# Delta-rule layer: the even halves of the merged blocks and the decayed keys are scaled on ScalarE instead of GpSimd

## The chip, the cores and the metric

The program runs on one core of one Trainium2 chip. The metric is the device time of one execution in microseconds. In the tables of the profile PE is TensorE (PEld its weight loads), DVE is VectorE, ACT is ScalarE, POOL is GpSimd and SP is SyncE, which issues the DMAs of this part.

## What is computed

A block of four mixers (convolution, softmax attention with forget gates, gated delta rule, sliding window) and then a second block, all on 512 positions and width 1024. The change lies in the gated delta rule alone, which is third. Cut to what matters:

```python
GDN_HEADS, GDN_HEAD_DIM, GDN_CHUNK = 8, 128, 64

def gdn_mixer(h, w_in, w_conv, a_log, dt_bias, w_onorm, w_out):
    proj = h @ w_in                                   # q, k, v, z, beta, a
    qkv = jax.nn.silu(causal_conv(qkv, w_conv))
    q = q * lax.rsqrt(jnp.sum(q * q, -1, keepdims=True) + EPS) * (1.0 / math.sqrt(d))
    k = k * lax.rsqrt(jnp.sum(k * k, -1, keepdims=True) + EPS)
    ...
    o = chunk_gated_delta(q, k, v, g, beta)
    o = o * lax.rsqrt(jnp.mean(o * o, -1, keepdims=True) + EPS) * w_onorm
    return (o.reshape(B_, S, GDN_WIDTH) * jax.nn.silu(z)) @ w_out

def chunk_gated_delta(q, k, v, g, beta):              # per head
    L = strict_lower((k * beta) @ k.T * decay)
    T = triangular_solve(eye + L, eye)                # inverse of a unit triangle
    u, w = T @ (v * beta), T @ (k * beta * exp(g_cum))
    k_dec = k * exp(g_last - g_cum)                   # the decayed keys
    def step(state, ...):
        v_new = u_c - w_c @ state
        o = (q * exp(g_cum)) @ state + qk_c @ v_new
        state = state * exp(gl) + k_dec.T @ v_new
```

## The kernel before

Activations lie feature-major, as eight tiles of 128 by 512. A projection from a weight column block is 24 matmuls of 128x512: for each of eight input tiles three products (lines 328 to 330), because both sides are split into a high and a low part (the weights by a cast on ACT, `whi`, and a subtraction on DVE, `wlo`). Such matmuls are called projection matmuls below.

`gdn_layer` goes through eight heads, with four blocks of 128 positions (NT = 4) where the chunks of 64 of the reference have become 128. For a head it projects, convolves and transposes the keys (`kt`), takes their norm (`ssk` on DVE, the power `rk` on POOL), scales them (`kn`, the tile `y`, line 765 on ACT), transposes them back (`knt`, then `knT`) and forms `kk`, the products of the keys with themselves. From these comes the strictly lower matrix `dc`. It is inverted in two parts.

`block_inverses` takes the 16x16 blocks on the diagonal: they are packed (`d1`, `d2`, line 870), sent to DRAM and read back spread over the partitions (the DMAs `dd` and `lb`), and solved column by column in 60 small DVE steps (lines 882 and 884), which leave `X`.

`unit_inverse_T` merges the blocks in three levels, s = 16, 32 and 64. At each level the new `X2` has an even half, which is the old X scaled by a column of ones and zeros (line 897), and an odd half, scaled likewise (line 918 on ACT; in the first level it is part of line 916 on DVE) and then corrected by products on TensorE (`Dt`, `z` and `e` in the first level, `dz` and `e` in the others). The tile of the last level is called `E`.

Then a recurrence over the four blocks: `ks` from the state S, `r` on DVE (line 812), `vn` from E and r, `ds` from the decayed `kn` (line 776 has scaled it by `kd`) and vn, the next S on DVE (line 824, the first one on ACT), and `o`. The outputs are scaled by `ro` (a power on POOL) into `on` (line 839), transposed (`ot`), and gated with `z`.

The instructions stand in program order on no engine: a scheduler lays out one in-order queue for each engine ahead of time from its own costs and the dependences. `issue_after` holds the inversion back until the projections of its head are issued, so that inversions and recurrences of one head lie between projections of the next. Each engine then works its queue strictly in turn, and an instruction that waits holds up all behind it.

Heads are numbered here from the first to the eighth. The program's own tile numbers (`X_6840`) are not the same in the two kernels.

Of the kernel before, what the change touches and what calls it, by code (L numbers as in the profile page):

```python
# [12 lines left out]
AF = mybir.ActivationFunctionType  # L13
# [5 lines left out]
P = 128  # L19
# [3 lines left out]
NT = 4  # L23
# [219 lines left out]
class KB:  # L243
# [419 lines left out]
    def gdn_layer(self):  # L663
        nc = self.nc
# [42 lines left out]
        v4 = lambda a: a.rearrange("p (t d) -> p t d", t=NT)  # L707
# [3 lines left out]
        blk = [slice(t * P, (t + 1) * P) for t in range(NT)]  # L711
# [26 lines left out]
        for hd in range(H):  # L738
# [6 lines left out]
            kd = self.small([P, NT], "kd")  # L745
# [17 lines left out]
            kn = kT  # L763
# [9 lines left out]
                c = blk[t]  # L773
                nc.vector.scalar_tensor_tensor(dc[:, c], kk[:, c], nb[:, t, hd:hd + 1], dc[:, c], ALU.mult, ALU.mult)
            X = self.block_inverses(dc)
            nc.gpsimd.tensor_mul(v4(kn)[:, :NT - 1], v4(kn)[:, :NT - 1], kd[:, :NT - 1].unsqueeze(2).to_broadcast([P, NT - 1, P]))

            vT, _ = conv_silu(2, hd)
            vps = self.t4(vT, "vt")
# [107 lines left out]
    def unit_inverse_T(self, N, X):  # L887

        nc = self.nc
        v4 = lambda a: a.rearrange("p (t d) -> p t d", t=NT)
        off = self.small([P, S], "off", 1)
        nc.gpsimd.tensor_mul(v4(off), v4(N), self.con("off16").unsqueeze(1).to_broadcast([P, NT, P]))
        for s in (16, 32, 64):
            X2 = self.big("E", shape=[P, NT, P]) if s == 64 else self.small([P, NT, 2 * s], f"X{2 * s}", 1)
            nc.gpsimd.tensor_scalar_mul(X2[:, :, :s], X, self.con(f"even{s}"))
            if s == 16:

                full = self.small([P, S], "full", 1)  # L900
                nb = P // s
                nc.vector.tensor_mul(full.rearrange("p (t b i) -> p t b i", t=NT, i=s), X.unsqueeze(2).to_broadcast([P, NT, nb, s]),
                                     self.con(f"bd{s}").rearrange("p (b i) -> p b i", i=s).unsqueeze(1).to_broadcast([P, NT, nb, s]))
                ps = self.t4(full, "Dt")
                Dm = self.small([P, S], "Dm", 1)
                nc.scalar.copy(Dm, ps)
                zp = self.att("z")
                z = self.small([P, NT * s], "zt", 1)
                for t in range(NT):
                    nc.tensor.matmul(zp[:, t * s:(t + 1) * s], off[:, t * P:(t + 1) * P], X[:, t], start=True, stop=True)  # L910
                nc.scalar.copy(z, zp[:, :NT * s])
                ep = self.att("e")
                for t in range(NT):
                    nc.tensor.matmul(ep[:, t * s:(t + 1) * s], Dm[:, t * P:(t + 1) * P], z[:, t * s:(t + 1) * s], start=True, stop=True)
                ev = ep[:, :NT * s].rearrange("p (t c) -> p t c", t=NT)
                nc.vector.scalar_tensor_tensor(X2[:, :, s:], X, self.con(f"odd{s}"), ev, ALU.mult, ALU.add)
            else:
                nc.scalar.activation(X2[:, :, s:], X, AF.Copy, scale=self.con(f"odd{s}"))
                dz = self.att("dz")
                Dz = self.small([P, S], "Dm", 1)  # L920
                rows = [(slice(r, r + s), slice(r, r + 2 * s)) for r in range(0, P, 2 * s)]
                w = NT * s
                for lo, pair in rows:
                    for t in range(NT):
                        c = slice(t * s, (t + 1) * s)
                        nc.tensor.matmul(dz[lo, c], X[pair, t], self.ident[pair, lo], start=True, stop=True)  # L926
                        c = slice(w + t * s, w + (t + 1) * s)
                        nc.tensor.matmul(dz[lo, c], N[pair, t * P + lo.start:t * P + lo.stop], X2[pair, t, s:], start=True, stop=True)  # L928
                    nc.scalar.copy(Dz[lo, :2 * w], dz[lo, :2 * w])
                ep = self.att("e")  # L930
                for lo, pair in rows:
                    for t in range(NT):
                        c = slice(t * s, (t + 1) * s)
                        nc.tensor.matmul(ep[lo, c], Dz[lo, c], Dz[lo, w + t * s:w + (t + 1) * s], start=True, stop=True)
                    nc.scalar.copy(X2[lo, :, s:], ep[lo, :w].rearrange("p (t c) -> p t c", t=NT))
            X = X2
        return X.rearrange("p t c -> p (t c)")
# [596 lines left out]
```

## Time and profile before

| | before |
|---|---|
| median of 3 runs | 2088.7 us (2084.69 to 2089.15) |
| the profiled execution | 2088.03 us, its span 2086.3 us |
| delta-rule heads, 505 to 905 us of the span | 400.0 us |
| PE, DVE, ACT, POOL busy in it | 371.4, 265.0, 236.4, 102.8 us |
| mean granted TensorE clock in it | 0.94 |

Busy time says how much an engine did. Which engine sets the time is read from TensorE's waits and from the granted clock: a matmul takes as many cycles in either case and twice as long at half clock.

### The profile page before, as it was taken

The numbers are of one execution on the slowest core, as the hardware profiler recorded it, in microseconds if no ns is written. First come the engines' busy times: TensorE is split into PE (matmuls) and PEld (weight loads), VectorE is DVE, ScalarE is ACT, GpSimd is POOL, SyncE is SP. The second block draws the span as 40 slices with busy tenths as digits, with TensorE's granted clock in tenths as the row PEclk, the third lists the DMA queues.
The fourth block names the chain that finished last, engine by engine and source line by source line (L and its number), as shares of the span: only waits on it lengthen the run. The fifth ranks groups of instructions, "written<-read, shape, count | busy, mean of one in ns | idle before, by whom it ended". The sixth has DMA issues, their size and how long they took to land.

```text
span 2086.3 us, 25930 instructions
## 1 busy us (share of the span) xinstructions
PE 2026.5 (97%) x9810; PEld 1592.0 (76%) x9810; DVE 1213.0 (58%) x2420; ACT 886.7 (43%) x1640; POOL 164.3 (8%) x178
## 2 busy tenths in 40 slices
PE   8999999999899988999999999999999999999999
PEld 6888787777777766778667767776788878888887
DVE  5545445555876765465765546644544467878621
ACT  4222343344776553453565454356622243322211
POOL 0000000000333221100001101000011100000000
PEclk9999999999999997999999999999999999999999
DMA  5233432225322221153114412120232342332331
GB/s 183 92 101 117 137 110 78 85 72 175 87 78 65 65 75 31 52 179 98 50 41 157 123 59 93 61 81 31 71 101 92 99 165 93 99 101 92 111 121 66
DMA packets 64508, 197.69 MB, mean 95 GB/s; under 512 B 8412, under 2 KB 8796, under 8 KB 64384
## 3 DMA queue, kind: packets, MB, share of 16 engines
q1 hardware_dynamic: 63440, 193.57, 28.9%
q0 software_dynamic: 800, 2.25, 0.4%
q8 instruction: 77, 1.26, 0.3%
q14 instruction: 47, 0.39, 0.1%
q10 hardware_dynamic: 144, 0.22, 0.0%
HBM read 183.13 MB, written 12.89 MB: 94 GB/s over the span
## 4 chain that ended last, share of the span: by engine, by line
PE 61%; DVE 5%; ACT 4%; DMA 2%; POOL 2%; issue 1%; POOLq 0%; SPq 0%; ACTq 0%; DVEq 0%
PE pj L330 16%; PE pj L328 16%; PE pj L329 16%; DMA lb<-dd 2%; PE s L1042 1%; PE z L1404 1%; DVE tmp L882 1%; PE o L1095 1%; PE pt L1086 1%; DVE X L884 1%; DVE wlo L223 1%; POOL rk L659 1%; PE dz L926 1%; PE tm L328 0%; PE dz L928 0%
## 5 line engine op out<-in xcount | busy, mean ns | idle before, releaser
L328 PE MATMUL pj<-hh,whi 128*128 128x512 f32 (+2 forms) x1528 | 609.1, 399 | 7.6 <-ACT hh L342 7.6
L329 PE MATMUL pj<-hl,whi 128*128 128x512 f32 (+2 forms) x1528 | 611.2, 400 | 1.2 <-DVE hl L343 1.2
L330 PE MATMUL pj<-hh,wlo 128*128 128x512 f32 (+2 forms) x1528 | 609.3, 399 | 2.0 <-DVE wlo L223 2.0
L222 ACT CAST whi<-raw 128x1024 fp32r<-128x1024 f32 x301 | 313.7, 1043 | 663.9 <-PE pj L329 417.3
L223 DVE TENSOR_TENSOR wlo<-raw,whi 128x1024 fp32r<-128x1024 f32 x301 | 375.5, 1248 | 203.5 <-ACT whi L222 197.2
L328 PEld LDWEIGHTS pj<-hh,whi 128*128 128x128 f32 (+2 forms) x1528 | 288.1, 189 | 68.3 <-ACT hh L342 8.0
L330 PEld LDWEIGHTS pj<-hh,wlo 128*128 128x128 f32 (+2 forms) x1528 | 288.3, 189 | 64.8 <-issue 4.3
L329 PEld LDWEIGHTS pj<-hl,whi 128*128 128x128 f32 (+2 forms) x1528 | 288.4, 189 | 62.7 <-issue 3.6
L328 PE MATMUL pj<-gh,whi 128*128 128x512 f32 x432 | 170.7, 396 | 0.5 <-ACT gh L339 0.3
L329 PE MATMUL pj<-gl,whi 128*128 128x512 f32 x432 | 170.7, 396 | 0.0
L330 PE MATMUL pj<-gh,wlo 128*128 128x512 f32 x432 | 170.6, 396 | 0.0
L634 DVE SCALAR_TENSOR_TENSOR y<-u,cols,y 128x512 f32<-128x512 f32 x160 | 123.0, 769 | 2.4
L328 PEld LDWEIGHTS pj<-gh,whi 128*128 128x128 f32 x432 | 81.0, 188 | 20.4 <-ACT whi L222 1.1
L329 PEld LDWEIGHTS pj<-gl,whi 128*128 128x128 f32 x432 | 81.0, 188 | 18.7 <-DVE gl L340 0.4
L330 PEld LDWEIGHTS pj<-gh,wlo 128*128 128x128 f32 x432 | 81.1, 188 | 18.4 <-DVE wlo L223 0.4
L473 DVE TENSOR_TENSOR x<-pj,x 128x512 f32<-128x512 f32 x48 | 33.1, 691 | 93.9 <-PE pj L330 93.9
L328 PE MATMUL pj<-whi,hh 128*128 128x512 f32 x168 | 66.4, 398 | 0.0
L329 PE MATMUL pj<-wlo,hh 128*128 128x512 f32 x168 | 66.1, 394 | 0.0
L330 PE MATMUL pj<-whi,hl 128*128 128x512 f32 x168 | 65.7, 392 | 0.0
L1435 DVE TENSOR_TENSOR gt<-pj,rb 128x512 f32<-128x512 f32 x24 | 16.5, 690 | 64.1 <-PE pj L330 64.1
L882 DVE TENSOR_TENSOR tmp<-lb,X 128x30 f32<-128x30 f32 (+14 forms) x240 | 43.7, 214 | 11.8 <-DMA lb<-dd 11.8
L1466 DVE TENSOR_TENSOR u<-pj,rb 128x512 f32<-128x512 f32 x44 | 30.5, 693 | 30.5 <-PE pj L330 28.7
(480 smaller groups left out, 2845.1 us busy)
## 6 DMA issues: line engine op xcount, KB each, us to landing
raw<-in_w_dram SPq DMA_DIRECT2D x290, 512.0 KB, 3.5
xd<-x SPq DMA_DIRECT2D x40, 256.0 KB, 2.0
x<-xd SPq DMA_DIRECT2D x40, 256.0 KB, 3.4
x<-in_xT_dram SPq DMA_DIRECT2D x16, 256.0 KB, 3.2
lb<-dd SPq DMA_DIRECT2D x8, 512.0 KB
raw<-in_w4m_dram SPq DMA_DIRECT2D x8, 512.0 KB, 4.0
ncb<-ncb SPq DMA_DIRECT2D x8, 256.0 KB
Gb<-Gb SPq DMA_DIRECT2D x8, 256.0 KB, 3.2
```

The costliest lines, as they stand in the source:

```text
L222: nc.scalar.copy(hi, raw)
L223: nc.vector.tensor_sub(lo, raw, hi.bitcast(F32))
L328: nc.tensor.matmul(out, ah, bh, start=start, stop=False)
L329: nc.tensor.matmul(out, ah, bl, start=False, stop=False)
L330: self.last = nc.tensor.matmul(out, al, bh, start=False, stop=stop)
L473: nc.vector.tensor_add(x, ps, x)
L634: nc.vector.scalar_tensor_tensor(y, u[:, t:t + S], self.col(f"{key}{t}", j), y, ALU.mult, ALU.add)
L659: nc.gpsimd.tensor_tensor(o, m, self.nhalf[:, :n], ALU.pow)
L882: nc.vector.tensor_mul(tmp[:, a, :n], lb[:, j + 1:, a, j].rearrange("p i t -> p t i"), X[:, a, j:j + 1].to_broadcast([P, 2, n]))
L884: nc.vector.tensor_add(X[:, a, j + 1:], X[:, a, j + 1:], tmp[:, a, :n])
L926: nc.tensor.matmul(dz[lo, c], X[pair, t], self.ident[pair, lo], start=True, stop=True)
L1466: nc.vector.tensor_mul(u[:, 2:], ps, self.rb)
```

## The change

In two places a multiplication by a column is taken from GpSimd and given to ScalarE, as an activation with a copy and a scale. The decayed keys were one GpSimd instruction on 128x384 and become three of 128x128. The even halves were one GpSimd instruction at each of three levels and remain one. For eight heads GpSimd gives up 32 instructions and ScalarE takes on 48. Lines behind line 776 stand one further down in the changed kernel.

```diff
@@ gdn_layer
             X = self.block_inverses(dc)
-            nc.gpsimd.tensor_mul(v4(kn)[:, :NT - 1], v4(kn)[:, :NT - 1], kd[:, :NT - 1].unsqueeze(2).to_broadcast([P, NT - 1, P]))
+            for t in range(NT - 1):
+                nc.scalar.activation(kn[:, blk[t]], kn[:, blk[t]], AF.Copy, scale=kd[:, t:t + 1])
@@ unit_inverse_T
             X2 = self.big("E", shape=[P, NT, P]) if s == 64 else self.small([P, NT, 2 * s], f"X{2 * s}", 1)
-            nc.gpsimd.tensor_scalar_mul(X2[:, :, :s], X, self.con(f"even{s}"))
+            nc.scalar.activation(X2[:, :, :s], X, AF.Copy, scale=self.con(f"even{s}"))
```

Since the scheduler lays out the queues anew, the order of all engines changes from the first head to the eighth; ahead of this layer and behind it the orders are the same. Nine loads of ScalarE's function table vanish in the layer and one is added. The number of other instructions stays.

ScalarE in the first head's merge, levels 32 and 64, before:

```order
L918 ACTIVATE X_4322<-X_4298,cons_c_3904 128x4x32
L929 COPY Dm_4326<-dz_4325 32x256 x2
L935 COPY X_4322<-e_4345 32x4x32 x2
L719 ACTIVATE y_4951<-y_4951 128x512
L918 ACTIVATE E_4356<-X_4322,cons_c_3904 128x4x64
```

and now:

```order
L898 ACTIVATE X_4324<-X_4300,cons_c_3904 128x4x32
L919 ACTIVATE X_4324<-X_4300,cons_c_3904 128x4x32
L751 ACTIVATE Gb_4903<-Gb_4903 128x512
L930 COPY Dm_4328<-dz_4327 32x256 x2
L222 CAST whi_5084<-raw_5082 128x1024
L936 COPY X_4324<-e_4347 32x4x32 x2
L898 ACTIVATE E_4358<-X_4324,cons_c_3904 128x4x64
L919 ACTIVATE E_4358<-X_4324,cons_c_3904 128x4x64
```

The even half (line 898) stands directly ahead of the odd half (line 919) at both levels.

VectorE from the seventh head's `d2` (line 870), behind which its DMAs leave, to the first steps of its solve (tiles `tmp` and `X`, which need `lb`), with `r` and `S` of the sixth head's recurrence between them, before:

```order
L870 TENSOR_TENSOR d_6834<-d_6828 128x64
L717 TENSOR_TENSOR u_3992<-pj_6957,rb_3922 128x512
L223 TENSOR_TENSOR wlo_7173<-raw_7170,whi_7172 128x1024
L812 SCALAR_TENSOR_TENSOR r_6676<-ks_6674,nbe_3989,y_6479 128x128
L630 TENSOR_SCALAR y_6983<-u_3992,cols 128x512
L634 SCALAR_TENSOR_TENSOR y_6983<-u_3992,cols,y_6983 128x512 x2
L824 SCALAR_TENSOR_TENSOR S_6684<-S_6669,eg_6288,ds_6682 128x128
L882 TENSOR_TENSOR tmp_6842<-lb_6838,X_6840 128x2x15 x2
L634 SCALAR_TENSOR_TENSOR y_6983<-u_3992,cols,y_6983 128x512
L812 SCALAR_TENSOR_TENSOR r_6692<-ks_6690,nbe_3989,y_6479 128x128
```

and now:

```order
L871 TENSOR_TENSOR d_6846<-d_6840 128x64
L634 SCALAR_TENSOR_TENSOR y_6997<-u_3992,cols,y_6997 128x512
L223 TENSOR_TENSOR wlo_7187<-raw_7184,whi_7186 128x1024
L787 TENSOR_SCALAR e_7003<-ss_7005 128x4
L813 SCALAR_TENSOR_TENSOR r_6688<-ks_6686,nbe_3989,y_6491 128x128
L792 TENSOR_TENSOR dT_6742<-kq_7011,dT_6742 128x512
L825 SCALAR_TENSOR_TENSOR S_6696<-S_6681,eg_6298,ds_6694 128x128
L813 SCALAR_TENSOR_TENSOR r_6704<-ks_6702,nbe_3989,y_6491 128x128
L883 TENSOR_TENSOR tmp_6854<-lb_6850,X_6852 128x2x15 x2
L885 TENSOR_TENSOR X_6852<-X_6852,tmp_6854 128x2x15 x2
```

The second `r` of the recurrence (`r_6692` before, `r_6704` now) stood behind the first solve step and stands ahead of it now.

VectorE in the third head's solve, with the second head's recurrence (`S`, `r`), before:

```order
L882 TENSOR_TENSOR tmp_5014<-lb_5010,X_5012 128x2x2 x2
L884 TENSOR_TENSOR X_5012<-X_5012,tmp_5014 128x2x2 x2
L882 TENSOR_TENSOR tmp_5014<-lb_5010,X_5012 128x2 x2
L884 TENSOR_TENSOR X_5012<-X_5012,tmp_5014 128x2 x2
L902 TENSOR_TENSOR full_5214<-X_5012,cons_c_3904 128x512
L824 SCALAR_TENSOR_TENSOR S_4856<-S_4841,eg_4460,ds_4854 128x128
```

and now:

```order
L883 TENSOR_TENSOR tmp_5018<-lb_5014,X_5016 128x2x10 x2
L885 TENSOR_TENSOR X_5016<-X_5016,tmp_5018 128x2x10 x2
L883 TENSOR_TENSOR tmp_5018<-lb_5014,X_5016 128x2x9 x2
L885 TENSOR_TENSOR X_5016<-X_5016,tmp_5018 128x2x9
L825 SCALAR_TENSOR_TENSOR S_4860<-S_4845,eg_4462,ds_4858 128x128
L885 TENSOR_TENSOR X_5016<-X_5016,tmp_5018 128x2x9
L883 TENSOR_TENSOR tmp_5018<-lb_5014,X_5016 128x2x8
L432 TENSOR_TENSOR z_5213<-pj_5188,rb_3922 128x512
L813 SCALAR_TENSOR_TENSOR r_4868<-ks_4866,nbe_3989,y_4655 128x128
```

The second head's recurrence has moved up: its second state stood behind the whole solve, and stands now behind the first 27 of its 60 steps. The wait for `lb` is that of the first step.

## Rows read from the trace of the kernel before

**Rows 1.** Windows: stretch, each engine's busy time (instructions), clock, DMA, GB/s.
```profile
505.00:905.00 400.00, 371.35 (x2247) 287.68 (x2246) 265.01 (x845) 236.38 (x544) 102.78 (x102) 0.94 0.25 72
```

**Rows 2.** Waits of PE, 505 to 905: total us, times, longest.
```profile
PE knt L642 <- ACT y L765: 6.7, 5, 3.0
PE ot L642 <- ACT on L839: 4.5, 3, 2.3
PE kt L642 <- ACT y L719: 4.2, 1, 4.2
PE vn L814 <- DVE r L812: 4.0, 1, 4.0
...
PE Dt L642 <- DVE full L902: 1.3, 1, 1.3
```

**Rows 3.** Lines of POOL, 505 to 905, then who waited for line 897.
```profile
L897 POOL TENSOR_SCALAR X<-X,cons_c 128x64 f32<-128x64 f32 (+1 forms) x16 | 14.7, 916 | 51.2 <-DVE X L884 33.5 <-DVE X L916 7.9 <-DVE rkm L657 7.0
...
L776 POOL TENSOR_TENSOR y<-y,kd 128x384 f32<-128x384 f32 x8 | 8.2, 1028 | 12.3 <-PE knt L642 12.3
L897 POOL TENSOR_SCALAR E<-X,cons_c 128x256 f32<-128x256 f32 x8 | 7.6, 944 | 39.7 <-ACT X L935 35.2 <-issue 4.5
...
  PEld dz L926: 0.9, 2
```

**Rows 4.** Timelines at 777 and 833: start us, length us, engine, instruction; DVE beside POOL.
```profile
776.98 0.94 POOL L897 TENSOR_SCALAR X<-X,cons_c 128x64 f32<-128x64 f32 x1 [3.35 <-DVE X L884]
776.91 0.69 DVE L902 TENSOR_TENSOR full<-X,cons_c 128x512 f32<-128x512 f32 x1
832.63 0.84 POOL L776 TENSOR_TENSOR y<-y,kd 128x384 f32<-128x384 f32 x1 [1.47 <-PE knt L642]
832.66 0.90 DVE L882 TENSOR_TENSOR tmp<-lb,X 128x4 f32<-128x4 f32 x2
```

**Rows 5.** Lines of ACT, 505 to 905: count, busy us, mean ns.
```profile
L719 ACT ACT_TABLE_LOAD x13 | 16.7, 1283 | 0.2
...
L918 ACT ACTIVATE E<-X,cons_c 128x256 f32<-128x256 f32 x8 | 4.0, 502 | 0.3
...
L918 ACT ACTIVATE X<-X,cons_c 128x128 f32<-128x128 f32 x8 | 3.2, 404 | 5.6 <-DVE rkm L657 2.8 <-DVE X L916 2.7
```

**Rows 6.** Timeline of PE at the two longest stops.
```profile
775.84 0.55 PE L642 MATMUL kt<-cons_c,y 128*128 128x128 f32 x3 [4.16 <-ACT y L719]
...
811.97 0.80 PE L814 MATMUL vn<-r,E 128*128 128x128 f32 x2 [3.97 <-DVE r L812]
```

**Rows 7.** Timeline of DVE: the seventh head's `d2`, and its first solve step.
```profile
799.63 0.22 DVE L870 TENSOR_TENSOR d<-d 128x64 f32<-128x64 f32 x1
...
810.68 0.31 DVE L882 TENSOR_TENSOR tmp<-lb,X 128x30 f32<-128x30 f32 x2 [4.60 <-DMA lb<-dd]
```

**Rows 8.** Windows behind short and long stops; the clock is the seventh column.
```profile
633.00:636.00 3.00, 3.00 (x14) 2.58 (x13) 2.36 (x16) 1.03 (x4) 0.94 (x1) 0.54 0.09 37
...
777.00:786.00 9.00, 8.34 (x32) 7.04 (x32) 4.52 (x8) 1.70 (x4) 2.02 (x3) 0.50 0.36 117
...
794.00:804.00 10.00, 10.00 (x61) 7.60 (x60) 3.88 (x10) 5.20 (x16) 2.02 (x2) 0.85 0.02 5
...
811.00:816.00 5.00, 4.03 (x16) 3.75 (x17) 3.35 (x22) 1.78 (x5) 0.00 (x0) 0.50 0.00 0
```

**Rows 9.** Timelines of ACT and PE, eighth head: from `kt` to `kn`, from `o` to `ot`.
```profile
828.27 0.60 ACT L760 ACTIVATE u<-kt 128x512 f32<-128x512 f32 x1 [0.74 <-PE kt L642]
...
831.20 1.15 ACT L765 ACTIVATE y<-kt,rk 128x128 f32<-128x128 f32 x4 [1.39 <-POOL rk L659]
887.31 0.49 PE L827 MATMUL o<-vn,dT 128*128 128x128 f32 x2
...
889.97 0.33 PE L642 MATMUL ot<-cons_c,on 128*128 128x128 f32 x1 [1.03 <-ACT on L839]
```

**Rows 10.** A window of projections alone, ahead of the layer.
```profile
480.00:500.00 20.00, 20.00 (x90) 16.57 (x89) 10.91 (x15) 6.83 (x11) 0.00 (x0) 1.00 0.57 191
```

## The prediction

> **What bounds the kernel now.** The change touches only the delta-rule heads, so I read the windows of that stage first. In its 400.0 us TensorE is busy for 371.4, VectorE for 265.0, ScalarE for 236.4 and GpSimd for 102.8, and the granted clock is 0.94 [rows 1]. TensorE is the bound, at 93%. What can be won or lost lies in two places: where TensorE stops, and where it then runs at half clock. Next, its waits. Almost all go back to ScalarE and VectorE: 6.7 us for the scaled keys before `knt`, 4.5 for `on` before `ot`, 4.2 for the silu before one `kt`, 4.0 for one `r` before `vn`, 1.3 for `full` before `Dt` [rows 2]. GpSimd is not among them. Then the timeline of the two long stops, 4.16 us at 775.8 and 3.97 us at 812.0 [rows 6], and the clock behind them: 0.50 at 777 to 786 and 0.85 over 794 to 804, which with the windows between makes about 20.5 us at half clock, and 0.50 again from 811 to 816, which goes on to about 821, 10.2 us [rows 8]. Short stops cost clock too: behind one of 1.67 us the window from 633 shows 0.54, some 3.4 us at the lower level [rows 8]. At half clock half the time is lost, so 3.4 us of it cost 1.7, 10.2 cost 5.1 and 20.5 cost 10.2.
>
> **What the moved instructions cost on their engines.** GpSimd loses eight times line 776 (8.2 us) and 24 times line 897 (14.7 + 7.6): 30.4 us [rows 3]. On the path that sets the end this is worth nothing by itself: TensorE waited for line 897 twice, 0.9 us in all, and the rows name nobody for line 776 [rows 3]. It is line 897 that waits, 51.2 and 39.7 us [rows 3].
>
> ScalarE gains 24 scalings of 128x128 at about 0.40 and 8 even halves each of 64, 128 and 256 columns. The odd halves of line 918 have the same forms: 0.404 and 0.502 [rows 5]; for 64 columns I estimate 0.35 by going on along that line. The sum is 24 x 0.40 + 8 x (0.35 + 0.40 + 0.50) = 19.6 us. Eight table loads fewer, at 1.283 each [rows 5], give back 10.3. The net is 9.3 us on an engine that stands idle for 400 - 236 = 164 us of the stage, so it hides, except where it stands in a chain that TensorE waits for. There are two such places. At levels 32 and 64 the even half now stands directly ahead of the odd half, so 0.40 and 0.50 come into the chain from X to the second product; in most heads two to four projections lie there, at 20.00/90 = 0.22 us each [rows 10], which hide it. And one or two of the key scalings stand ahead of the copy to `knT` in some heads, 0.4 to 0.8 us. Bounds for the two together: 0 and 8 x (0.9 + 0.8) = 13.6 us. I take **+1**, near the lower end, since the waits name no odd half and no `kk`.
>
> **Contention.** While line 776 ran at 832.6 two solve steps on VectorE took 0.90 us [rows 4], against 0.31 for two elsewhere [rows 7]. So GpSimd's two-tensor work slows VectorE. Line 897 doesn't: at 777.0 it ran for 0.94 beside `full`, which took 0.69 [rows 4], as all eight of them do (0.68 to 0.69). Eight times 0.6 would be 4.8 us off VectorE, which is the bound on that side; not every one of the eight lies beside VectorE's work, and little of that is in a chain. Between 0 and -4.8 I take **-1.5**.
>
> The Trainium skill, "SBUF — State Buffer", section "SBUF: two separate sides", says of this that VectorE and GpSimd share a port pair as an exclusive lock, and that whoever starts first keeps it for the whole instruction while the other fully blocks. By that rule line 897 would have held up `full` and the steps of the solve as well; the row at 777 doesn't show it. The rule's result is the second rival below.
>
> **What the new order does.** This is the larger part: all five queues are laid out anew. I follow the places where TensorE waited before, and where it could now.
>
> Seventh head. Its `d2` is done at 799.85 and its `lb` lands at 810.7, 10.8 us later [rows 7]; `r` of the sixth head stood behind that wait, hence the stop of 3.97 [rows 6]. Now two `r` and one S stand ahead of the first solve step. The stop and its half clock go: -3.97 - 5.1 = **-9.1**. What is late next is the third `r`, some 16 us of TensorE work behind `kk`, about when `lb` comes; I take no stop there.
>
> Sixth head. The stops of 4.16 and 1.27 [rows 2, 6] with 20.5 us at half clock [rows 8]: the convolution of the next keys stood behind the solve on VectorE. Now 12 projections lie between `kt` and `Dt` instead of none, and the gate stands ahead of the solve; but `d2` comes about 1.6 us later, and `lb` takes as long as before. Bounds: 0 and -5.4 - 10.2 = -15.6. I take two smaller stops of 2 us each with 3.4 us at half clock, that is 4 + 3.4 against 15.6: -8.2, and of this **-5**, because the later `d2` speaks for more than 2 us.
>
> Keys. From `kt` to `knt` the scaling needs at least 828.27 to 831.6, 3.3 us (square, norm, power, first scaling) [rows 9]. The projections between the two, counted in the order for the eight heads, were 25, 12, 16, 15, 11, 12, 9, 10 and are 25, 10, 9, 9, 13, 11, 12, 13. Nine are 2.0 us, so the third and fourth heads, with 16 and 15 before, now stop for over a microsecond each; the fifth and eighth gain some of it. I add 1.6 to the 6.7 us of waiting [rows 2], and the 1.7 of one short stretch at half clock: **+3.3**.
>
> Outputs. From the last `o` to `ot` the chain needs 887.8 to 889.9, 2.1 us at the least (square, power on GpSimd, scaling) [rows 9], and some 3 in most heads. The projections between were 7, 10, 13, 12, 10, 9, 9, 5 and are 3, 12, 7, 6, 5, 6, 4, 3: 29 fewer, 6.4 us of cover. With the small matmuls that lie there too the covers now sum to an estimated 14.6 us. Head by head against a chain of 2.1 that leaves 4.9 us of waiting, against one of 3.0 it leaves 10.8; before it was 4.5 [rows 2]. Between +0.4 and +6.3 I take **+3**.
>
> Third head. The second state of the second head's recurrence now stands behind 27 steps of the solve. From `d2` to `lb` it is 10.8 us, and 27 steps at 0.31 for two make 4.2 at the most [rows 7]; with some 3 us from `kk` to `d2` S is ready about 16 to 18 us behind `kk`. TensorE has 41 projections there, 9.1 us [rows 10], and the merge's and the recurrence's small matmuls, together an estimated 15 to 20 us. That is 0 to 2.2 of waiting, with clock up to +4: **+1**.
>
> Tail. The eighth head's even half of level 16 stands on ScalarE ahead of the seventh's `Dz` copy and waits for the eighth's solve; by the same prices both are due an estimated 25 us behind `kk`, so this is 0 to +3: **+0.5**.
>
> **Sum.** +1 - 1.5 - 9.1 - 5 + 3.3 + 3 + 1 + 0.5 = -6.8 us, from the profiled execution's 2088.0 (span 2086.3 and 1.7 around it) to 2081.2. The median of the runs lies 0.7 higher, so I say **2082**.
>
> **Rivals.** *A solve carries other waits* (slower). `lb` comes 10 us behind `d2` whatever the order, and VectorE works its queue in turn. If `lb` lands in the third head later than TensorE's 15 to 20 us cover, S and the whole recurrence stop there as `r` did before: 4.0 + 5.1 instead of 1, +8. If the stop of the sixth head also remains, with its long half clock, +5 for the gain that fails. That gives 2082 + 13 = 2095, and 2100 where the half clock lasts 20 us instead of 10. It decides from some 3 us of lateness. For it: VectorE stood still for 4.60 us at such a wait [rows 7]; against it: the recurrence of the seventh head now stands clear of it.
>
> *VectorE is freed* (much faster). If every microsecond of the moved instructions (30.4) [rows 3] had held VectorE up, then without them its chains (`r`, `full`, the convolution of the keys) come early enough that both long stops go with all their half clock: -5.4 - 10.2 - 9.1 = -24.7, and with the +8 of shorter covers and stops about 2071, at best 2064. The same time would follow if the new order simply suits. Against it: line 897 beside an unstretched `full` [rows 4]. The lock of the Trainium skill's page "SBUF — State Buffer" is what would make it so.
>
> *Nothing* (same). GpSimd wasn't waited for, ScalarE has room, and gains and losses of the order cancel: 2088.
>
> **How the numbers follow.** A measurement of this kernel can tell some 0.2%, 4.2 us, from no change: 2084.5 to 2092.9 is the same. My forecast (2077 to 2087) has 0.38, of which 0.08 reaches into the same; VectorE freed (2064 to 2077) 0.12; nothing (2085 to 2092) 0.19; the slower rival (2092 to 2103) 0.31. Faster 0.30 + 0.12 = 0.42, the same 0.27, slower 0.31. With both signs likely the range must reach from 2066 to 2102; the forecast's own is 2077 to 2087.
>
> **What would show it.** Right: no stop of `vn` for `r` in the seventh head, no stretch of half clock over 10 us between the sixth and seventh heads, waits for `knt` of 8 to 9 us and for `ot` of 5 to 11 us, ScalarE's busy time up by 9 us, GpSimd's down by 30, waits for even halves under 1 us. Wrong: a stop of 3 us or more for S, `r` or `kt` behind the wait for `lb`, with a stretch of half clock behind it; or odd halves and `kk` among TensorE's waits with several microseconds, by which ScalarE's additions were in the chain after all.

## The result: slower, at 2101.15 us

The changed kernel takes 2101.15 us at the median (2092.62 to 2101.86), the kernel before 2088.70 on the same chip: a ratio of 1.0055, interval 1.0038 to 1.0072, or about +11.5 us. The time lies outside the forecast's own range of 2077 to 2087. It is inside the wide range of 2066 to 2102, which allowed for both signs, close to its upper end. The sign was forecast wrong, and it is the time of the slower rival. The profiled execution took 2101.86, the longest of the five; its span is 2100.1, so against the span of before (2086.3) it shows +13.8 us.

First the stretch of the delta-rule heads, as in [rows 1] (20 us longer, since the stage ends later), with the same window of before under it, and what TensorE waited for in it, as in [rows 2]:

```profile
505.00:925.00 420.00, 388.54 (x2276) 300.16 (x2276) 264.27 (x851) 243.15 (x587) 69.56 (x70) 0.92 0.25 73
505.00:925.00 420.00, 391.35 (x2333) 303.89 (x2332) 276.40 (x860) 243.95 (x554) 104.01 (x104) 0.95 0.27 80
```

```profile
PE knt L642 <- ACT y L765: 7.4, 5, 2.9
PE ot L642 <- ACT on L840: 6.9, 6, 1.9
PE kt L642 <- ACT y L719: 6.3, 3, 3.1
PE Dt L642 <- DVE full L903: 2.6, 2, 1.5
PE pj L328 <- ACT gh L339: 2.2, 1, 2.2
...
PE vn L815 <- DVE r L813: 0.7, 1, 0.7
```

The long stop for `r` is gone, 4.0 to 0.7. Instead `kt` waits three times and not once, `Dt` twice, `ot` six times and not three, and the projection behind the heads waits for `gh`. All stops together grow by 3.3 us (table below). The clock falls: its mean over the 420 us is 0.92 and was 0.95. The stops on TensorE's timeline (start, length, instruction; in brackets the idle time before it and who ended it):

```profile
693.04 1.12 PE L642 MATMUL kt<-cons_c,y 128*128 128x128 f32 x4 [3.06 <-ACT y L719]
...
782.33 0.66 PE L642 MATMUL kt<-cons_c,y 128*128 128x128 f32 x4 [2.41 <-ACT y L719]
...
786.83 0.66 PE L642 MATMUL Dt<-cons_c,full 128*128 128x128 f32 x4 [1.11 <-DVE full L903]
789.98 0.33 PE L642 MATMUL knt<-cons_c,y 128*128 128x128 f32 x1 [2.49 <-ACT y L765]
...
852.26 0.25 PE L927 MATMUL dz<-cons_c,X 64*32 64x32 f32 x2 [0.46 <-DVE X L917]
...
904.50 1.65 PE L328 MATMUL pj<-gh,whi 128*128 128x512 f32 x3 [2.15 <-ACT gh L339]
```

In [rows 6] there were two such stops, of 4.16 and 3.97. Now windows behind the new ones, and with 840 to 852 one ahead of a fall of the clock (TensorE's busy time is the second number, the granted clock the seventh column, as in [rows 8]):

```profile
692.00:699.00 7.00, 5.96 (x17) 4.85 (x17) 7.00 (x28) 2.80 (x6) 1.52 (x1) 0.51 0.25 77
791.00:811.50 20.50, 20.50 (x112) 15.53 (x111) 6.22 (x13) 9.36 (x26) 1.32 (x2) 0.50 0.06 16
840.00:852.00 12.00, 11.51 (x68) 9.29 (x66) 9.32 (x29) 4.28 (x8) 2.38 (x2) 1.00 0.62 157
852.50:866.00 13.50, 13.50 (x69) 8.94 (x69) 7.81 (x55) 4.55 (x11) 0.00 (x0) 0.50 0.09 26
903.70:910.50 6.80, 6.00 (x14) 4.74 (x15) 4.09 (x7) 4.50 (x7) 0.00 (x0) 0.50 0.21 77
```

The 20.5 us at half clock, which the prediction wanted to see gone, are still there at 791. At 852.5 a new stretch of 13.7 us begins with hardly a stop ahead of it; in before the clock was 1.00 from 821 to the end of the layer. In the layer and its tail the stretches at half clock make 64.8 us, and made 44.3.

The engines, from the list of ScalarE's lines and the page's busy times, against [rows 3, 5]:

```profile
L777 ACT ACTIVATE y<-y,kd 128x128 f32<-128x128 f32 x24 | 9.2, 410 | 0.0
...
L898 ACT ACTIVATE E<-X,cons_c 128x256 f32<-128x256 f32 x8 | 4.0, 505 | 0.1
...
L898 ACT ACTIVATE X<-X,cons_c 128x64 f32<-128x64 f32 x8 | 2.8, 350 | 8.8 <-DVE X L885 8.8
```

```profile
PE 2038.0 (97%) x9810; PEld 1599.4 (76%) x9810; DVE 1208.1 (58%) x2420; ACT 890.9 (42%) x1680; POOL 130.6 (6%) x146
```

With 3.2 us for the halves of 128 columns (402 ns each) the additions sum to 9.2 + 4.0 + 3.2 + 2.8 = 19.2 us. Before, PE was busy for 2026.5, DVE 1213.0, ACT 886.7 and POOL 164.3. ScalarE works 4.2 us longer, GpSimd 33.7 less, VectorE 4.9 less; TensorE, with the same 9810 matmuls, 11.5 us longer.

**Where the 13.8 us are.** I took each matmul's time to the start of the next one, less a stop between them, and compared it with the mean of the same tile's matmuls at full clock over the ten traces of this study that have no added matmuls. What is over in a half-clock stretch is its cost; what is over elsewhere is how the small matmuls lie among the wide ones. For the heads and their tail, from the profiled executions (us):

| kernel | span less before's | lost at half clock (us at half clock) | stops | rest | added matmuls | sum less before's |
|---|---|---|---|---|---|---|
| before | 0 | 18.3 (44.3) | 26.2 | -0.8 | | 0 |
| after | +13.8 | 26.4 (64.8) | 29.5 | +1.7 | | +13.9 |
| e1: new operations, old order | +4.1 | 18.9 (44.3) | 27.9 | +0.4 | | +3.5 |
| e2: old operations, new order | +5.5 | 17.7 (40.9) | 31.2 | +0.7 | | +5.9 |
| e3: only the keys | +9.0 | 19.5 (47.7) | 33.4 | +0.1 | | +9.3 |
| e4: only the even halves | -6.3 | 9.3 (27.2) | 27.7 | +1.7 | | -5.0 |
| e5: whole change, order of e4 | -6.7 | 6.5 (17.0) | 27.5 | +2.1 | | -7.6 |
| e9: old operations, order of e4 | -11.1 | 7.4 (20.4) | 26.2 | 0.0 | | -10.1 |
| e7: after, stops filled | +4.3 | 11.9 (30.7) | 29.9 | +1.5 | 5.9 | +5.5 |
| e11: e4, stops filled | -13.5 | 5.2 (13.6) | 13.7 | -0.6 | 13.1 | -12.3 |

The sum follows the span within 1.3 us in every row. So between these two executions the change costs 8.1 us of clock, 3.3 of stops and 2.5 of looser spacing. A microsecond at half clock costs 0.41 (18.3 / 44.3 and 26.4 / 64.8), and 0.34 to 0.43 in the other rows.

Behind each row stands one execution, and the clock differs from one to the next. After's row is its execution with the lowest mean clock: 0.983 at 2101.86 us, while its fastest has 0.992 at 2092.62. So the 8.1 us of clock belong to the lowest clock of five executions, and the experiments below are judged by their medians and intervals.

### The profile page after: what moved, and what is told of

Same layout as the page of the kernel before. It is cut to its first block, busy times and chain, and to the rows that moved or that the text cites. A ratio compares the mean times of both kernels' runs of the same rounds, so it can differ in the third digit from the quotient of the medians.

```text
span 2100.1 us, 25919 instructions
## 1 busy us (share of the span) xinstructions
PE 2038.0 (97%) x9810; PEld 1599.4 (76%) x9810; DVE 1208.1 (58%) x2420; ACT 890.9 (42%) x1680; POOL 130.6 (6%) x146
## 4 chain that ended last, share of the span: by engine, by line
PE 51%; ACT 3%; DVE 2%; issue 1%; POOL 1%; POOLq 0%; ACTq 0%; DVEq 0%
PE pj L329 14%; PE pj L330 14%; PE pj L328 14%; PE s L1043 1%; PE z L1405 1%; PE o L1096 1%; PE pt L1087 1%; PE tm L328 0%; PE s L1313 0%; ACT e L1388 0%; PE o L1410 0%; PE tm L330 0%; PE tm L329 0%; PE num L1323 0%; PE o L1224 0%
## 5 line engine op out<-in xcount | busy, mean ns | idle before, releaser
L634 DVE SCALAR_TENSOR_TENSOR y<-u,cols,y 128x512 f32<-128x512 f32 x160 | 121.0, 757 | 2.2
```

What stands on the lines that cost most here:

```text
L634: nc.vector.scalar_tensor_tensor(y, u[:, t:t + S], self.col(f"{key}{t}", j), y, ALU.mult, ALU.add)
```

## Experiments: the operations or the order?

The theory after the result: the move between engines costs next to nothing, and the order that the scheduler laid out anew costs the time, by stops and by the half clock behind them. The rival: ScalarE's additions stand in chains that TensorE waits for. The order can be held: behind the traced layer every instruction of an engine's recorded queue gets an order-only edge to the one ahead of it, and only the moved instructions are left free (the code is shortened).

```
for i, prev in zip(queue[1:], queue):     # one engine's queue, as recorded
    tc.add_manual_dep(i, prev.name, DependencyInfo(NoSync, DATA), reason="pinned")
```

**e1.** The new operations with all queues of the layer in the order of before.

> The changed instructions (keys and even halves on ScalarE), but every engine's queue of the delta-rule layer held in the order of the kernel before; only the moved instructions find their own place. Theory A, the new order costs the time (its stops and the half clock behind them): no slower than before, ratio 0.997 to 1.002, the stops of 4.2 us before kt and of 4.0 us before vn are back, and the half clock at 777 to 797. Rival B, the additions on ScalarE stand in the chain that TensorE waits for: 2096 to 2104, ratio about 1.005, with several microseconds of new waits for knt, kk or dz.

Measured: 2089.37 us, ratio 1.0015 (1.0006 to 1.0023), +3.1 us. Its stops on TensorE's timeline are those of before again, the one for `r` shorter (2.65 for 3.97):

```profile
780.08 0.90 PE L642 MATMUL kt<-cons_c,y 128*128 128x128 f32 x3 [4.27 <-ACT y L719]
...
815.16 0.49 PE L815 MATMUL vn<-r,E 128*128 128x128 f32 x2 [2.65 <-DVE r L813]
```

with one wait in TensorE's list that before did not have among its larger ones:

```profile
PE kk L771 <- ACT knT L768: 1.1, 2, 0.7
```

That is the key scalings ahead of the copy to `knT`, at the size which the prediction gave as their bound. So in this order some 3 of the 11.5 us are the operations' (1.3 to 4.8 by the interval). Holding the order costs nothing by itself: e6 below, held in the order of before with the old operations and one instruction moved, has the ratio 1.0001.

**e2.** The other way round: the operations of before, in the order of after.

> The reverse: the instructions of before (keys and even halves on GpSimd), every queue of the layer held in the order of the changed kernel, and the moved instructions find their own place on GpSimd. Theory A (order): 2092 to 2104, ratio about 1.005, with TensorE's three stops before kt and the half clock behind 852 as in the changed kernel. Rival B (ScalarE's additions): about 2088, ratio 0.998 to 1.002.

Measured: 2097.41 us, 1.0058 (1.0044 to 1.0071). The order alone gives the loss, with GpSimd at 163.7 us again. Its stops stand where after's do:

```profile
691.98 0.66 PE L642 MATMUL kt<-cons_c,y 128*128 128x128 f32 x4 [2.82 <-ACT y L719]
...
781.01 0.66 PE L642 MATMUL kt<-cons_c,y 128*128 128x128 f32 x4 [2.50 <-ACT y L719]
```

and the windows at 789 and 852:

```profile
789.00:809.50 20.50, 20.50 (x113) 15.52 (x111) 6.23 (x13) 7.61 (x21) 4.08 (x5) 0.50 0.06 22
852.00:866.00 14.00, 14.00 (x119) 10.23 (x118) 7.92 (x52) 5.55 (x14) 2.88 (x3) 1.00 0.14 39
```

A stop of 2.23 for `knt` stands at 788.67 too. In this execution, the fastest of the kernel's, the clock did not fall at 852. Its profile shows +5.5, and the median is 11.2 above before's: this execution's mean clock is 0.989, that of the two slowest (2101.2) 0.985 and 0.986. Where it fell in those isn't recorded.

**e3 and e4.** The two halves of the change, each with the order that the scheduler makes of it: `for t in range(NT - 1): nc.scalar.activation(kn ...)` alone, and `nc.scalar.activation(X2[:, :, :s], ...)` alone.

> Only the decayed keys go to ScalarE (24 instructions of 0.40 us in place of eight on GpSimd); the queues are laid out anew. By rival B (additions in the chain) the two halves of the change add up: at most 24 x 0.40 = 9.6 us slower, some 2 to 4 us likely, ratio 1.001 to 1.002. By theory A the time has little to do with these instructions: anything from 2070 to 2105, and TensorE's stops and half-clock stretches account for the difference to within 2 us.

> Only the even halves go to ScalarE (24 instructions, about 10 us); the queues are laid out anew. By rival B most of the 12 us stay, since the even halves lie between the solve and the levels of the merge: 2095 to 2100. By theory A anything from 2070 to 2105, with the difference again accounted for by stops and half-clock stretches, and no relation to the sum of the two halves.

Measured: 2098.49, 1.0070 (1.0050 to 1.0090), and 2077.53, 0.9964 (0.9952 to 0.9976). Opposite signs: +14.6 and -7.5, which add up to +7.1 where both together give +11.5. In e4 no `kt`, `Dt` or `vn` makes a long stop, and the clock between the sixth and seventh heads stays up, with more busy time on ScalarE (248.4) than after has in 20 us more:

```profile
505.00:905.00 400.00, 370.44 (x2272) 287.80 (x2271) 267.42 (x851) 248.44 (x573) 80.82 (x78) 0.97 0.25 76
765.00:800.00 35.00, 31.87 (x223) 25.05 (x222) 23.51 (x84) 20.43 (x52) 6.48 (x7) 1.00 0.23 72
```

TensorE is as idle as before (370.44 busy against 371.35 [rows 1]); what makes it faster is the clock, 0.97 for 0.94.

**e5 and e9.** Is e4 faster for its operations or for its order? The whole change, and none of it, in the order of e4.

> The whole change (keys and even halves on ScalarE), with every queue of the layer held in the order of the kernel that moves the even halves only (2077.5 us); the key scalings find their own place. Theory A (the order sets the time): 2075 to 2083, faster than before by 0.2 to 0.5%, with no stop before kt, Dt or vn of the fifth to seventh heads and no stretch of 20 us at half clock. Rival B (ScalarE's additions cost what they take in its chains): the keys alone were 12 us slower, so 2088 to 2098.

> The instructions of before (keys and even halves on GpSimd) with every queue of the layer held in the order of the kernel that moves the even halves only. With the two runs on that order it closes a table of three orders by which engine does the scalings. Theory A (order sets the time): 2074 to 2082, ratio 0.994 to 0.998, as fast as that kernel although nothing has moved to ScalarE. Rival B (that kernel was faster since GpSimd no longer holds VectorE, or since the even halves come earlier on ScalarE): 2084 to 2090, ratio 0.999 to 1.002.

Measured: 2081.27, 0.9972 (0.9962 to 0.9982), and 2077.75, 0.9959 (0.9944 to 0.9973). So by three orders and what runs in them:

| order | scalings on GpSimd | even halves on ScalarE | both on ScalarE |
|---|---|---|---|
| of before | 1 | | 1.0015 |
| of after | 1.0058 | | 1.0055 |
| of e4 | 0.9959 | 0.9964 | 0.9972 |

Along a row the time moves by -0.6 to +3 us, down a column by 8 to 21. So ScalarE's additions fall as the cause of the loss.

**e10.** Is any new order as large a change? This was to be the control: the kernel before, with the GpSimd scaling of the keys written behind the next convolution, so that the scheduler lays the queues out once more.

> A control: the kernel before with no instruction on another engine; only the line that scales the keys on GpSimd is written behind the next convolution instead of ahead of it, so that the scheduler lays the queues out once more (some 5% of TensorE's rows move). If a new order alone moves the time by as much as the change did (theory A), anything from 2075 to 2102 is possible and a difference of over 4 us would not surprise. If orders are worth little (rival B): within 2 us of before.

Measured: 2087.78, 1.0002 (0.9994 to 1.0011). But the order is not a new one. The two programs hold the same instructions in the same order in every engine's queue, and the two traces show the same 9810 matmuls one behind the other. The twentieth of the rows that seemed to move are rows whose tiles have a number one lower. So e10 is the kernel before a second time and a measure of scatter: `vn` waits 4.6 us where before has 4.0, `knt` 7.6 for 6.7, and the stretches at half clock make 40.9 us for 44.3, with the two long ones at the same places. Differences of this size between two rows of the table say nothing. Whether most new orders cost or win time stays untested; the three orders above lie 8 to 21 us apart.

## Experiments: the stops and the clock behind them

**e6.** The largest term of the prediction, -9.1, was that `r` leaves its place behind the wait for `lb`. Here that alone: the order of before, one `r` moved three places up on VectorE, ahead of the seventh head's first solve step (difference of the two orders on VectorE).

```
+L812 SCALAR_TENSOR_TENSOR r_6692<-ks_6690,nbe_3989,y_6479 128x128
 L882 TENSOR_TENSOR tmp_6842<-lb_6838,X_6840 128x2x15 x2
 L634 SCALAR_TENSOR_TENSOR y_6983<-u_3992,cols,y_6983 128x512
-L812 SCALAR_TENSOR_TENSOR r_6692<-ks_6690,nbe_3989,y_6479 128x128
```

> The kernel before with every queue held, and one instruction moved: on VectorE the second r of the sixth head's recurrence stands ahead of the seventh head's first solve step, three places earlier, as the changed kernel has it. It prices the first term of my sum alone. As predicted (stop of 3.97 and 10.2 us at half clock go): -9 us, ratio 0.9957. Rival C (the clock falls all the same, or the stop comes back at the next r or state): -4 us or less, ratio 0.998 to 1.000.

Measured: 2086.78, 1.0001 (0.9992 to 1.0009): nothing. The waits for `r` are gone from the list, and TensorE stops 1.6 us later for what also stood behind `lb`, the last step of the convolution of the queries (L634 in the rows above), by way of `u` and `ss`:

```profile
813.56 0.59 PE L853 MATMUL ss<-cons_c,u 128*128 128x1 f32 x2 [4.49 <-ACT u L850]
```

Behind it the clock is at half for 10.2 us, as before. A wait on a queue is a wait of everything behind it. In after all of these stand ahead of the solve, and `ss` waits 0.3.

**e7.** Does the half clock come from the stops? After's order, and ahead of the stops of the sixth and seventh heads matmuls of 128x512 in TensorE's idle time, 10 before `kt`, 4 before `Dt`, 10 before `knt`. As in the other kernels with such matmuls, they write a tile which the following ones overwrite, so that nothing computed hangs on them.

```
+nc.tensor.matmul(ps, h[0][0][:, :P], h[0][0], start=True, stop=True)   # n times, ps is the tile's own
```

> The changed kernel in its own order, with 24 extra matmuls of 128x512 (0.22 us each) on TensorE that write the tile that is overwritten right behind them: 10 ahead of the seventh head's kt, 4 ahead of the sixth head's Dt, 10 ahead of the seventh head's knt. They stand where TensorE waited 2.4, 1.1 and 2.5 us, and bring no result earlier. Theory D (what costs is the half clock behind the stops): the 20.5 us at half clock from 791 go, and the time falls by some 10 us, to 2088 to 2093. Rival E (the waiting itself costs): the time stays or rises by what doesn't fit, 2099 to 2104.

Measured: 2091.55, 1.0024 (1.0014 to 1.0034), by the two ratios 6.5 us under after, although its list of waits still holds 9.1 for `knt` and 6.9 for `ot`. The 20.5 us at half clock, which after, e2 and e12 all have, are gone; the stretch of the eighth head remains:

```profile
780.00:800.00 20.00, 18.53 (x136) 14.04 (x134) 11.21 (x33) 10.74 (x30) 2.77 (x3) 1.00 0.17 54
843.40:857.00 13.60, 13.22 (x69) 8.75 (x70) 8.43 (x60) 4.76 (x11) 0.00 (x0) 0.50 0.08 15
```

Against after's profile 14.5 us of clock are saved, 9.5 of them at this place, for 5.9 us of added matmuls. The other 5 us lie at places where nothing was added, so they are scatter between executions. Of the three stops here `kt`'s is down to 0.28 us, `Dt`'s stays at 1.20, `knt`'s is gone, and the clock stays up: the half clock here came of the stops.

**e8.** The same in the order of before: 16 ahead of `kt`, 4 of `Dt`, 15 of the `vn` that waits.

> The kernel before in its own order, with 35 such matmuls: 16 ahead of the seventh head's kt (stop of 4.16 us), 4 ahead of the sixth head's Dt (1.27), 15 ahead of the sixth head's third vn (3.97). Theory D: the stretches of 20.5 and 10.2 us at half clock go, -15 us, 2070 to 2075, ratio about 0.993. Rival E: no gain, 2086 to 2092.

Measured: 2084.17, 0.9987 (0.9978 to 0.9996), -2.7: a miss by much. Half clock falls from 44.3 to 20.4 us, but the 15 matmuls for `vn` cannot start before the tile is free (it shares its buffer with `ks`, which `r` reads), so they waited for the same `r` and then ran ahead of the product:

```profile
805.77 5.30 PE L848 MATMUL vn<-hh 128*128 128x512 f32 x15 [2.56 <-DVE r L812]
810.91 0.38 PE L814 MATMUL vn<-r,E 128*128 128x128 f32 x2
```

The stop stayed and the recurrence came later. As a test of the clock at `vn` this run is inconclusive. At `kt` it agrees with e7 in part: the stop there is down to 0.58 us and the clock stays at 1.00 behind it, but from 782, around a stop of 1.04 us for `knt`, it is at half for 10.2 us all the same.

**e12.** The stretch at 852.5 has no stop of weight ahead of it (0.46 at most), but many small matmuls. 10 wide ones ahead of the seventh head's `Dt`, some 5 us before:

> The changed kernel in its own order with 10 extra matmuls of 128x512 ahead of the seventh head's Dt, where TensorE did not stop but went over to narrow matmuls, and where the clock fell 5 us later for 13.7 us. If the clock falls there because of the narrow matmuls, the stretch is gone from the profile and the time is 2094 to 2100 (10 x 0.22 us lost, 5 us won in the runs that had it). If it falls for the pauses of 0.3 and 0.5 us behind, it falls again and the time is 2100 to 2104.

Measured: 2098.01, 1.0056 (1.0041 to 1.0071). The window of the eighth head's merge, right behind the added matmuls:

```profile
850.00:864.00 14.00, 14.00 (x114) 9.79 (x113) 10.00 (x64) 5.69 (x14) 1.09 (x1) 1.00 0.24 80
```

The clock stays at 1.00 where after has 0.50, but the ratio is after's. Since e2, without added matmuls, also ran once without this fall, the one profile does not show that they removed it, and the median does not show a gain.

**e11.** The order of e4 with its remaining stops filled (12 and 5 ahead of two `knt`, 36 ahead of five `ot`):

> The kernel that moves the even halves only, in its own order, with 53 extra matmuls of 128x512 at seven of its stops (12 and 5 ahead of the first and second heads' knt; 5, 6, 7, 12 and 6 ahead of the first, third, fourth, fifth and eighth heads' ot). Theory D (the half clock behind a stop can be kept off by keeping TensorE busy): two or three of its short stretches at half clock go, 2072 to 2076, ratio about 0.994. Rival E: what is filled in doesn't fit or the clock falls elsewhere, 2077 to 2084.

Measured: 2074.96, 0.9945 (0.9930 to 0.9959), under both kernels and at the level of e4 and e9 or a little below. Stops in the heads fall from 27.7 to 13.7, but the 53 matmuls take 13.1 themselves; what is left of the gain is again clock, 5.2 us lost at the lower level for 9.3 (table above).

## Why the sign was wrong, step by step

Stops and clock of before and after, from the two profiles (clock by the cost of each stretch, as in the table above):

| step of the prediction | forecast | stops | clock | together |
|---|---|---|---|---|
| ScalarE's additions, contention | -0.5 | | | +3.1 (e1), -0.6 (after against e2) |
| seventh head, `r` behind `lb` | -9.1 | -3.3 | -4.1 | -7.4 |
| sixth head, `kt` and `Dt` | -5 | +0.6 | +0.4 | +1.0 |
| keys, `knt` (less the 2.49 counted one row up) | +3.3 | -1.8 | 0 | -1.8 |
| outputs, `ot` | +3 | +2.4 | +1.7 | +4.1 |
| third head, S (`ks`) and its `Dt` | +1 | +0.2 | -1.3 | -1.1 |
| tail, an even half ahead of the `Dz` copy | +0.5 | no wait | | 0 |
| projection behind the heads, `gh` | not listed | +1.9 | +2.4 | +4.3 |
| fifth head, `kt` | not listed | +3.1 | +2.4 | +5.5 |
| second head, `kt` | not listed | +0.9 | +1.4 | +2.3 |
| eighth head, from 852 | not listed | +0.5 | +5.3 | +5.8 |

The rows add up to the clock's 8.1 us (8.2 with rounding) and, less about 1 us of small stops elsewhere that went, to the stops' 3.3.

**Right.** The prices on the engines: 19.2 us of additions against 19.6, 0.350 for the 64 columns that were an estimate, nobody on TensorE waiting for an even half. The stop for `r` went, with 7.4 of 9.1 us, though not by `r`'s new place alone, which in e6 was worth nothing. `ot` waits 6.9 (5 to 11 forecast).

**Right by luck, or without effect.** `knt` waits 7.4, near the 8 to 9 forecast, but 2.49 of it belong to the sixth head's stops, and in the third and fourth heads, on which the term of +3.3 rested, it waits less than 0.25 and 0.72. VectorE's busy time is less by 4.9, the bound given for contention, and by 4.2 in e1 with the order held (1208.8 for 1213.0); no time came of it there, where the ratio is 1.0015. ScalarE's busy time grew by 4.2 rather than 9: in a held order the additions lengthen it by 13.4 (e1 against before) and 14.2 (after against e2), less than the sum of their lengths, and eight table loads fewer give back 10.3.

**The step that failed: the sixth head, -5.** Two stops of 2 us, with 3.4 us of half clock behind each, were taken; there came three, of 2.41, 1.11 and 2.49, with 20.5 us, and in place of -5 the table has +1.0. Twelve projections now lie between `kt` and `Dt`, and after them TensorE stood again. VectorE shows why; the rows run from the landing of `lb` to `full`, without idle time:

```profile
768.06 0.72 DVE L883 TENSOR_TENSOR tmp<-lb,X 128x30 f32<-128x30 f32 x2 [0.55 <-DMA lb<-dd]
...
772.05 1.43 DVE L885 TENSOR_TENSOR X<-X,tmp 128x28 f32<-128x28 f32 x2
...
777.90 0.68 DVE L717 TENSOR_TENSOR u<-pj,rb 128x512 f32<-128x512 f32 x1
...
786.10 0.68 DVE L903 TENSOR_TENSOR full<-X,cons_c 128x512 f32<-128x512 f32 x1
```

From 768.06 to 786.78 VectorE is the bound: the solve, two convolutions and the gate all pass through it, and whichever the scheduler puts first, another one is later. As I read it, a new order shares these 19 us out, and whether TensorE stands then is a matter of what it has left to do there; no run tests this alone. In after it stood three times, in e4 not at all. The prediction read this place as a matter of who stands behind whom, and saw only the wait for `lb`, which here is 0.55 us.

**The steps that were missing.** They weigh more than the one that failed. The prediction followed the places where TensorE had waited. Three of the places that cost most had no stop of weight in before (0.30 at the most), and the sum put them at nothing: the fifth head's `kt`, the eighth head from 852 and the projection behind the heads, together 15.6 us. This is read from the two executions; no run changes one of these places alone. In the fifth head it is the slower rival's mechanism, a solve that stands ahead of what others need, but in another head and by another cause than the rival named, by steps in work and not by a late `lb`. VectorE, and GpSimd beside it:

```profile
683.25 1.30 POOL L743 TENSOR_TENSOR dc<-cons_c,Gb 128x512 f32<-128x512 f32 x1 [3.43 <-DMA Gb<-Gb]
683.29 1.31 DVE L885 TENSOR_TENSOR X<-X,tmp 128x28 f32<-128x28 f32 x1
684.52 1.44 DVE L883 TENSOR_TENSOR tmp<-lb,X 128x26 f32<-128x26 f32 x2
...
688.62 0.68 DVE L717 TENSOR_TENSOR u<-pj,rb 128x512 f32<-128x512 f32 x1
```

The convolution of the keys (L717, then L634 until 692.3) starts behind 35 of the 60 solve steps. VectorE waits 0.96 us for the transfer of `Gb` among them, and the three steps that run beside GpSimd's L743 and L744 take 1.31 and 1.44 us, where two take 0.30 elsewhere. The silu and `kt` follow at 693.04. In the third head, where the rival put its stop, S came in time (0.4).

**The rivals.** *A solve carries other waits* gave 2095 to 2100 and is nearest: a solve did carry others, and the sixth head's stop and long half clock did remain, which it had as its second condition. *VectorE is freed* fell as a price of time: it would have made e2, with 33 us of GpSimd's scalings back beside VectorE, slower than after; the ratios are 1.0058 and 1.0055, and VectorE's busy times 1208.8 and 1208.1. The exclusive lock itself is seen in part. In the rows of the fifth head VectorE's step at 683.29 ends with GpSimd's L743 (684.60 and 684.55), and in [rows 4] the first of the two steps beside line 776 lasts from 832.66 to 833.49, where that line ends at 833.47. Line 897 did not hold the solve up so: of nine steps beside it at 593.29 to 594.30 in before, eight took 0.17 to 0.19 us and one 0.38. But the row at 777 is no evidence against a lock, as the prediction took it. There `full` began 0.07 us ahead of line 897, and it was line 897 that took 0.94 us; all seven that ran beside a `full` took 0.94 to 1.00, and the one that ran alone took 0.45:

```profile
695.30 0.45 POOL L897 TENSOR_SCALAR X<-X,cons_c 128x64 f32<-128x64 f32 x1
```

Of this the Trainium skill, "SBUF — State Buffer", section "SBUF: two separate sides", has the rule that whoever starts first keeps the shared ports for the whole instruction. The rows of `full`, of line 776 and of L743 agree with it, those of line 897 beside the solve don't.

*Nothing* holds for the engines alone, not for the kernel.

**What stays open.** Why the spacing of the matmuls at full clock is 2.5 us looser in after was not separated. The fall of the clock at 852 came in after and e7, and not in the profiles of e2 and e12; after's times scatter by 9 us (e2's by 8), the slow ones at the lower mean clock, and how much of that is this one stretch isn't shown. That the stops made the half clock is shown for the sixth head alone (e7); for the fifth head and the projection behind the heads it is inferred from the order in time.

## What to carry over

A change of engine under a scheduler is two changes: hold the order and move the operations, then hold the operations and move the order, before a cause is looked for in either. In costing a new order, walk through all places where an engine in demand is busy without a break, not only those where somebody waited before, and for a wait that goes list everything that stood behind it. A stop of TensorE costs its own length and often half clock behind it, and the second can be the larger part: in the sixth head 6.0 us of stops and 9.5 of clock.

## What was not expected of the hardware

**Half clock costs less than half.** In the half-clock stretches of before and after 0.41 us are lost per microsecond, not the 0.5 of the prediction: in after a projection takes 0.26 us on average at full clock and 0.47 at half, from its start to the next one's, but a `dz` of the merge 0.057 and 0.087 and an `e` 0.069 and 0.095. "Twice as long", as said ahead of the prediction, is nearly so for the projections and too much for the small matmuls.

**The clock can fall with hardly a stop.** From 840 to 852 TensorE was busy for 11.51 of 12 us, with 0.46 us as its longest pause; from 844.9 on 36 small matmuls (`ss`, `kq`, `Dt`, `z`, `e`) lay among 11 projections. Then the clock stood at half for 13.7 us; in e2, with a pause of 0.92 us at the same place, it did not fall. After stops of 1 to 3 us it was 3.4, 6.8 or 20.5 us, and in e7 a stop of 3.03 us for the fifth head's `kt` left it as it was.

**Useless matmuls can pay.** 24 of them, 5.9 us, made after faster by some 6.5 us (e7).
